# Seven products for the first group of two attention pairs, with its neighbours moved

## The chip, the cores and the metric

The kernel runs on one core of one Trainium2 chip. Its time is the device time of one execution in microseconds (us), the median of three runs. The core has a matrix engine (TensorE, "PE" in the profile; "PEld" is its weight load), a vector engine (VectorE, "DVE"), a scalar engine (ScalarE, "ACT"), GpSimd ("POOL") and SyncE ("SP"). ACT, DVE and POOL each take their instructions in the order of one queue. In this kernel SP and POOL also issue the transfers (DMA). PE accumulates in eight PSUM banks of 128 x 512 words.

## The reference

Two layers on 512 tokens of width 1024. Layer one is attention with eight heads of 128 in three groups of windows: group 0 looks back over 128 neighbouring tokens, group 1 over 128 tokens at distance 4, group 2 over 128 tokens at distance 16. Each group has its own q, k and v. The first 32 of the 128 dimensions of q and k are turned by position (rope). The three groups' outputs are joined with weights from their log sum of exponentials:

```
for g, (window, dilation) in enumerate(((128, 1), (512, 4), (2048, 16))):
    q = rope(proj[:, :, g, 0]) * scale;  k = rope(proj[:, :, g, 1]);  v = proj[:, :, g, 2]
    o, lse = dilated_window_attention(q, k, v, window, dilation)
wts = softmax(stack(lses), axis=0);  out = einsum(wts, stack(outs)) @ w_out
```

Then come a gated feed-forward layer, a recurrent mixer (mLSTM) with its own feed-forward layer, and a last norm. Only the attention of layer one is changed.

## The kernel before

Everything is float32. A float32 product is made of three matmuls in a rounded format: each operand is split into a high part, a rounded copy made by ScalarE (`split_chunk`, L223), and a low part, the remainder, made by VectorE (L225); then high x high, high x low and low x high are summed in PSUM (`SPLITS`). A block of weights is 128 x 1024 words, 512 KB. It is fetched into one of three buffers by SP, cast, and its remainder taken. Split blocks have four buffers, so a few blocks can be ready before PE needs them; `Feed` holds the list of blocks to come (`plan`) and those that are ready, and `feed.ahead` says how many.

Attention works on four pairs of heads (`pr` 0 to 3), and for each pair on the groups 0, 1, 2 in turn. For each, q and k of the two heads are projected from the normed input. There are two ways to do it:

- plain (`project`): q and k, each 2 blocks x 2 heads x 4 chunks x 3 matmuls, in all 96 matmuls of 512 columns;
- by seven products (`qk_unit`): the 2 x 2 block product of Strassen in Winograd's form. Sums of the input blocks (S1 to S4) are made once before. Each group then takes seven products of 24 matmuls of 256 columns, in the order P1, P5, P6, P2, P7, P3, P4 (`QK_ORDER`), on four differences of weight blocks (L879, made by VectorE in `prepare_part`) and with copies and sums of the results (L911 to L931).

Before the change, pair 0 is plain in all groups, pairs 1 to 3 have a plain group 0 and seven products in groups 1 and 2. In the program's names a2g0q is q of pair 2, group 0, and a2g1c, a2g1p, a2g1u are the accumulators of its group 1. Group 0 holds its q and k in an order by blocks of tokens, the other two in token order by classes.

After a group comes its turn by position (`rope`): the first 32 rows are packed on ACT (L905), turned on DVE (L607 to L616) and copied back (L628 by ACT for groups 1 and 2; POOL for group 0).

The attention of a pair (`attention_pair`) is cut into steps that run between the projections of later groups. A counter, the tick, is raised four times in every group (`advance`; in a group of products after P5, P2, P3 and P4), and `defer(n, fn)` puts a step n ticks on. So a pair of projections lasts twelve ticks. The steps, with their ticks before the change, counted from the start of the next pair's projections:

- `scores0` (group 0): 16 matmuls, masks and maxima on DVE (L709), exponentials on ACT (L753). It runs in its own pair, `SCORES0_AT` = 6 ticks after that pair's group 0, that is at tick 10, after P2 of group 2. Casts that are queued after it in the program are placed behind its exponentials on ACT (`ahead_of_casts`), low parts behind its last DVE instruction (`ahead_of_splits`).
- `scores12` (groups 1 and 2), tick 1: 32 matmuls, 16 masked maxima of 128 columns on DVE (L737), exponentials on ACT (L758).
- `joint`, tick 4: the three groups' maxima and sums are exchanged and joined into factors; `weigh(0)`, 4.5, and `weigh(1)`, 8: the probabilities of a head are multiplied by their factors on DVE (L802, L805), eight instructions each.
- `transposes(0)`, 5, and `transposes(1)`, 8; the results go to memory and come back (`bring`), 7 and 9.
- `values(0)`, 11, and `values(1)`, 12: 30 matmuls each (L829, L834), whose result is kept in memory by `keep_head`. `load_values` (2, 3 and 1) fetches the v that they need; it has one buffer.

The order on PE is fixed: `run` puts a step's matmuls together at its place, and the next product's matmuls follow it (`fenced`). On the other engines the instructions are placed by a planner, mostly in the order of the program, with the constraints named above. Pair 3 has no next pair: its steps run beside the projection of the last values (a3g12v, four blocks) by `LAST_AT`; then comes the output projection (awo), for which the kept heads 0 to 5 are fetched by `bring_heads`.

Of the kernel before, what the change touches and what calls it, by code (L numbers as in the profile page):

```python
# [35 lines left out]
SCORES0_AT = 6  # L36
RUN_AT = (1, (4, 4.5, 5, 7, 8, 8, 9), (11, 12), (2, 3, 1))
LAST_AT = (1, (2,), (), (1, 1, 1))
# [35 lines left out]
def tile_hybrid_dilated_attn_mlstm(  # L74
# [329 lines left out]
    with ExitStack() as actx:  # L404
# [9 lines left out]
        mask_band, mask_causal, mask_dil, perm = part(K_MA, 2 * P), part(K_M1, P), part(K_M2, P), part(K_G, P)  # L414
        cosn = ap.tile([P, SEQ], F32, name="cosn")
# [242 lines left out]
        def attention_pair(pr, qks):  # L658
# [35 lines left out]
            def scores0(q, k):  # L694
# [26 lines left out]
                else:  # L721
                    defer(2, lambda: behind(exps, engine=ACT))
# [3 lines left out]
            def scores12(gs=(1, 2)):  # L726

                for g in gs:
# [6 lines left out]
                for g, i in [e for e in ((1, 0), (2, 0), (1, 1), (2, 1)) if e[0] in gs]:  # L735
# [5 lines left out]
                    if g == 2:  # L741
                        exponentials(1, i)

            def exponentials(o, i):

                if o:
                    nc.vector.tensor_tensor(own[:, 0, 1, i], mx[:, 0, i], mx[:, 1, i], op=ALU.max)
# [49 lines left out]
            def weigh(i):  # L797
                cf4 = weight[0]
                for b in range(4):
                    pb = max(2 * b - 1, 0)  # L800
                    blk = p0[i][:, pb:2 * b + 1, :].rearrange("p a b -> p (a b)")
                    nc.vector.tensor_scalar(blk, blk, cf4[:, 0, i, b:b + 1], None, op0=ALU.mult)  # L802
                for c in range(4):
                    blk = p12[i].rearrange("p (g c) k -> p c g k", g=2)[:, c]
                    nc.vector.tensor_scalar(blk, blk, cf4[:, 1, i, c:c + 1], None, op0=ALU.mult)  # L805
# [58 lines left out]

        def load_part(pr, g, key):
            if g > 2:
                return
# [6 lines left out]
        def prepare_part(pr, g, name):  # L874
# [21 lines left out]
        def qk_unit(pr, g, qk):  # L896
# [7 lines left out]
            def pack(q, src):  # L904
                nc.scalar.activation(two_m(rot[0][quarter(q)]), src, AF.Copy)  # L905

            def finish(name):
# [8 lines left out]
                elif name in ("P2", "P4"):  # L916
                    th = int(name == "P4")
                    src = two_m(acc[target[name]])
                    if th == 0:
                        t = ap.tile([P, 2, SEQ], F32, tag="rot", name="rot")  # L920
                        rot = t[:, 0], t[:, 1]
                    pack(th, src[:R])
# [1470 lines left out]
```

## Time and profile before

| | |
|---|---|
| median of three runs | 1385.5 us (1385.12 to 1385.57) |
| the profiled execution | 1385.26 us, span of the trace 1383.5 us |
| attention's pairs 1, 2 and 3 (from the trace) | 179.6 to 255.7, 255.7 to 332.1, 332.1 to 410.05 us |
| last values, output projection | to 434.2, to 484.7 us |

Rows of the profile read as follows. A timeline row has the start in us from the start of the span, the duration, the engine, the line of the kernel, the operation, the tile written and the tiles read, the shape, how many were merged (x3), and in brackets how long the engine was idle before it and what ended that. A row of busy time by stretch has the stretch, its length, then for each engine its busy time and its number of instructions, then the granted clock of PE, the share of the transfer engines and GB/s. A row of a group by line has the number of instructions, their busy time, the mean duration of one in ns, and the idle time of the engine before them. PE's matmuls overlap one another: the distance from one start to the next is what a matmul costs, not its duration.

### The profile page before, as it was taken

What the parts mean: (1) busy time and instruction counts of PE and PEld (TensorE: products, weight loads), DVE (VectorE), ACT (ScalarE), POOL (GpSimd) and SP (SyncE); (2) the same over time, 40 slices, a digit from 0 to 9 for tenths busy, and PEclk for the clock granted to TensorE, in tenths of its full rate; (3) what the DMA queues carried; (4) which work ended last, traced back from release to release, by engine and by line L of the source; (5) the groups of instructions that cost most, each with busy time, mean ns of one, the idle gap of its engine ahead of it and who ended that gap; (6) DMA issues with size and microseconds to landing.
All of it is one profiled execution on the core that took longest, in us unless ns stands there. A gap on an engine that the chain in (4) does not pass through costs nothing. (4 is left out here: it accounts for less than half of the span.)

```text
span 1383.5 us, 22546 instructions
## 1 busy us (share of the span) xinstructions
PE 1368.5 (99%) x8740; PEld 1242.9 (90%) x8740; DVE 1111.3 (80%) x1845; ACT 780.5 (56%) x1246; POOL 180.2 (13%) x264
## 2 busy tenths in 40 slices
PE   9999999999999999999999999999999999999997
PEld 7888889899998889999999998898888999999886
DVE  7758769696896489788778798898858988887887
ACT  6556565656554354444476464695534454448854
POOL 3000013121211010000010110122102330001113
PEclk9999999999999999999999999999999999999999
DMA  8534255637286256323362742324335553335863
GB/s 298 176 120 139 77 153 161 197 122 237 91 280 205 102 137 183 111 73 122 122 153 77 168 124 80 103 66 119 92 122 124 156 173 105 122 122 129 192 167 100
DMA packets 140067, 193.81 MB, mean 140 GB/s; under 512 B 8980, under 2 KB 104788, under 8 KB 139960
## 3 DMA queue, kind: packets, MB, share of 16 engines
q1 hardware_dynamic: 119552, 139.81, 31.7%
q0 software_dynamic: 18752, 51.43, 15.7%
q8 instruction: 69, 1.13, 0.3%
q10 hardware_dynamic: 1656, 1.12, 0.2%
q14 instruction: 38, 0.31, 0.1%
HBM read 167.30 MB, written 22.54 MB: 137 GB/s over the span
## 5 line engine op out<-in xcount | busy, mean ns | idle before, releaser
L1696 POOL DMA_DIRECT2D f1T<-in_ffn_w_out_dram x15 | 17.8, 1185 | 208.7 <-DMA f1P_2w_w<-in_ffn_w_out_dram 135.7
L1671 POOL DMA_DIRECT2D f0S<-in_ffn_w_out_dram x10 | 8.7, 874 | 260.3 <-DVE f0hid L1588 173.1
L2228 POOL DMA_DIRECT2D hD<-hB x32 | 21.7, 697 | 68.3 <-DVE hB L2225 68.3
L255 PE MATMUL mo<-n_h,mo_k_l 128*128 128x512 f32 x64 | 25.3, 396 | 0.0
L255 PE MATMUL mo<-n_h,mo_k_h 128*128 128x512 f32 x64 | 25.3, 395 | 0.0
L255 PE MATMUL mo<-n_l,mo_k_h 128*128 128x512 f32 x64 | 25.2, 393 | 0.0
L255 PE MATMUL awo<-ao_h,awo_k_h 128*128 128x512 f32 x64 | 25.2, 393 | 0.0
L255 PE MATMUL mqk<-n_h,mqk_k_h 128*128 128x512 f32 x64 | 25.1, 392 | 0.0
L255 PE MATMUL mwo<-yo_l,mwo_k_h 128*128 128x512 f32 x64 | 25.1, 392 | 0.0
L255 PE MATMUL mqk<-n_l,mqk_k_h 128*128 128x512 f32 x64 | 25.1, 392 | 0.0
L255 PE MATMUL f0j<-n_h,f0j_h 128*128 128x512 f32 x64 | 25.0, 391 | 0.0
L255 PE MATMUL f1j<-n_h,f1j_h 128*128 128x512 f32 x64 | 25.0, 391 | 0.0
L255 PE MATMUL awo<-ao_h,awo_k_l 128*128 128x512 f32 x64 | 25.0, 391 | 0.0
L255 PE MATMUL mwo<-yo_h,mwo_k_l 128*128 128x512 f32 x64 | 25.0, 391 | 0.0
L255 PE MATMUL mqk<-n_h,mqk_k_l 128*128 128x512 f32 x64 | 25.0, 390 | 0.0
L255 PE MATMUL awo<-ao_l,awo_k_h 128*128 128x512 f32 x64 | 25.0, 390 | 0.0
L255 PE MATMUL f0j<-n_h,f0j_l 128*128 128x512 f32 x64 | 24.9, 390 | 0.0
L255 PE MATMUL f1j<-n_h,f1j_l 128*128 128x512 f32 x64 | 24.9, 390 | 0.0
L255 PE MATMUL f0j<-n_l,f0j_h 128*128 128x512 f32 x64 | 24.9, 389 | 0.0
L255 PE MATMUL f1j<-n_l,f1j_h 128*128 128x512 f32 x64 | 24.9, 389 | 0.0
L255 PE MATMUL mwo<-yo_h,mwo_k_h 128*128 128x512 f32 x64 | 24.8, 391 | 0.0
L225 DVE TENSOR_TENSOR v1P_l<-v1W,v1P_h 128x1024 fp32r<-128x1024 f32 x14 | 17.1, 1222 | 9.3 <-ACT v1P_h L223 9.3
(2613 smaller groups left out, 5875.7 us busy)
## 6 DMA issues: line engine op xcount, KB each, us to landing
f0j_w<-in_ffn_w_in_dram SPq DMA_DIRECT2D x17, 512.0 KB, 4.8
f1j_w<-in_ffn_w_in_dram SPq DMA_DIRECT2D x17, 512.0 KB, 6.4
f1T<-in_ffn_w_out_dram POOLq DMA_DIRECT2D x15, 512.0 KB, 7.0
f0hid<-in_ffn_w_in_dram SPq DMA_DIRECT2D x9, 512.0 KB, 5.2
f1hid<-in_ffn_w_in_dram SPq DMA_DIRECT2D x9, 512.0 KB, 4.8
v0W<-in_attn_w_in_dram SPq DMA_DIRECT2D x8, 512.0 KB, 6.1
v1W<-in_attn_w_in_dram SPq DMA_DIRECT2D x8, 512.0 KB, 3.5
awo_k_w<-in_attn_w_out_dram SPq DMA_DIRECT2D x8, 512.0 KB, 4.5
```

The lines of the kernel that those rows point to most:

```text
L225: nc.vector.tensor_tensor(lo[:, :n], raw[:, :n], hi[:, :n].bitcast(F32), op=ALU.subtract)
L255: nc.tensor.matmul(acc, whl[a][:, k, m * P:(m + 1) * P], pairs[b][kk], start=(kk == 0 and (a, b) == SPLITS[0]), stop=(kk == nk - 1 and (a, ...
L1671: nc.gpsimd.dma_start(t, src[1][:, ks], accum_op=ALU.add)
L1696: nc.gpsimd.dma_start(view(to), weight_rows(hk * UNITS + u, n), accum_op=ALU.add)
L2228: nc.gpsimd.dma_start(hD[k // 4].rearrange("(b i) x -> i b x", i=R)[:, :, c0:c0 + R], t[R * a_:R * (a_ + 1)])
```

## The change

Group 0 of pairs 2 and 3 is projected by seven products as well (`PRODUCTS_FROM = 2`, `by_products`). The weights of that group are fetched while group 2 of the pair before is prepared. Its results are written in the order by blocks, so each copy and sum is done once per head (`each`), its packed rows lie in two tiles of another pool, and the turned rows go back by POOL.

For all pairs but the last, `weigh(1)` runs on ACT instead of DVE, and at tick 7 instead of 8.

`scores12`, where it does both groups, takes the maximum over both groups at once (`both_groups`): eight instructions of 256 columns instead of sixteen of 128 and a maximum of the two; the exponentials follow after all of them. Pair 3 keeps the old way.

`scores0` runs one tick later, after P3 of group 2. The values run at 14.4 and 15.4, that is in the next pair's group 0 after P2 and P3 (for pair 2, beside the last values' projection), and `load_values` at 4, 5 and 4. In pair 3 the exponentials of `scores0` are put off by one tick instead of two, and heads 4 and 5 are fetched four ticks after heads 0 to 3.

```
-SCORES0_AT = 6
-RUN_AT = (1, (4, 4.5, 5, 7, 8, 8, 9), (11, 12), (2, 3, 1))
-LAST_AT = (1, (2,), (), (1, 1, 1))
+SCORES0_AT = 7
+RUN_AT = (1, (4, 4.5, 5, 7, 7, 8, 9), (14.4, 15.4), (4, 5, 4))
+PRODUCTS_FROM = 2
+LAST_AT = (1, (2,), (), (4, 4, 4))
...
-            for ks in (slice(0, 4), slice(4, 6)):
+            def bring_some(ks):
                 nc.sync.dma_start(t[:, ks], oD[ks].rearrange("k p s -> p k s"))
+            bring_some(slice(0, 4))
+            defer(4, lambda: bring_some(slice(4, 6)))
...
-                    defer(2, lambda: behind(exps, engine=ACT))
+                    defer(1, lambda: behind(exps, engine=ACT))
...
+            def both_groups():
+                for c2 in range(2):
+                    for i in range(2):
+                        sp = banks_[c2, i] = score_bank(i, "%ss12" % nm)
+                        for c in (2 * c2, 2 * c2 + 1):
+                            for g in (1, 2):
+                                q, k = qks[g]
+                                sl, o = slice(c * P, (c + 1) * P), (c % 2 * 2 + g - 1) * P
+                                nc.tensor.matmul(sp[:, o:o + P], q[:, i, sl], k[:, i, sl], start=True, stop=True)
+                two_g = lambda t: t.rearrange("p (g k) -> p g k", g=2)
+                for i in range(2):
+                    for c in range(4):
+                        nc.vector.tensor_tensor_reduce(
+                            p12[i].rearrange("p (g c) k -> p c g k", g=2)[:, c],
+                            two_g(banks_[c // 2, i][:, c % 2 * 2 * P:(c % 2 + 1) * 2 * P]), two_g(mask_both),
+                            1.0, -3e38, op0=ALU.add, op1=ALU.max, accum_out=own[:, 0, 1, i, c:c + 1])
+                ahead_of_splits[0] = last_on(DVE)
+                for i in range(2):
+                    exponentials(1, i)
...
+                def times(blk, f):
+                    if i and pr < HEADS // 2 - 1:
+                        nc.scalar.activation(blk, blk, AF.Copy, scale=f)
+                    else:
+                        nc.vector.tensor_scalar(blk, blk, f, None, op0=ALU.mult)
...
+        def by_products(pr, g):
+            return pr > 0 and (g > 0 or pr >= PRODUCTS_FROM)
...
             if g > 2:
+                pr, g = pr + 1, 0
+            if pr == HEADS // 2:
                 return
...
+            follows = g < 2 or pr + 1 >= PRODUCTS_FROM
             if name == "P7":
                 less("W21", "W21", "W11")
                 for key in ("W11", "W12"):
-                    load_part(pr, g + 1, key)
-            elif name in ("P3", "P4"):
+                    if follows:
+                        load_part(pr, g + 1, key)
+            elif name in ("P3", "P4") and follows:
                 load_part(pr, g + 1, src)
...
+            def each(out, src, th, fn):
+                if g:
+                    fn(halves(out, th), *(two_m(t) for t in src))
+                    return
+                for m in range(2):
+                    at = slice(m * HALF, (m + 1) * HALF)
+                    fn(in_order(out[:, m])[:, :, 2 * th:2 * th + 2],
+                       *(t[:, at].rearrange("p (c b j) -> p b c j", c=2, b=TB) for t in src))
...
-                    pack(th, src[:R])
-                    nc.scalar.activation(halves(qk[0], th), src, AF.Copy)
+                    pack(th, two_m(src[:R]))
+                    each(qk[0], [src], th, lambda to, x: nc.scalar.activation(to, x, AF.Copy))
...
-                    pack(2 + th, out[:R])
+                    if g:
+                        pack(2 + th, halves(qk[1], th)[:R])
+                    else:
+                        for m in range(2):
+                            nc.scalar.activation(packed(rot, 2 + th, m, True), turned(qk, 2 + th, m, True), AF.Copy)
...
-                if pr and g:
+                if by_products(pr, g):
                     qk.extend(tok_tile("%sg%d_%s" % (nm, g, "qk"[part])) for part in range(2))
-                    qk_unit(pr, g, qk)
+                    qk_unit(pr, g, qk, then if g == 0 else None)
                     continue
```

More of the change, by code (lines that the diff above doesn't have):

```diff
@@ L414, in tile_hybrid_dilated_attn_mlstm @@
         mask_band, mask_causal, mask_dil, perm = part(K_MA, 2 * P), part(K_M1, P), part(K_M2, P), part(K_G, P)
+        mask_both = part(K_M1, 2 * P)
         cosn = ap.tile([P, SEQ], F32, name="cosn")
@@ L967, in qk_unit @@
                 if n == 6 and not last:
-                    back = rope(qk, rot, False)
-                    if g == 2:
+                    back = rope(qk, rot, g == 0)
+                    if g == 0:
+                        defer(1, lambda: back(True))
+                    elif g == 2:
                         back()
@@ L975, in qk_unit @@
                     advance()
+                if n == 6 and then is not None:
+                    then()
                 if n:
@@ L1240, in tile_hybrid_dilated_attn_mlstm @@
             for g, part, ch in itertools.product(range(3), range(2), range(2)):
-                if pr and g:
+                if by_products(pr, g):
                     if (part, ch) == (0, 0):
```

25 lines of the change are left out of this document (15 added, 10 removed).

## The prediction

> **What bounds the kernel now.** I read the page first, then busy time by stage for pair 2, then the timelines of PE, ACT and DVE there, and last the groups by line.
>
> ```profile
> span 1383.5 us, 22546 instructions
> ...
> PE 1368.5 (99%) x8740; PEld 1242.9 (90%) x8740; DVE 1111.3 (80%) x1845; ACT 780.5 (56%) x1246; POOL 180.2 (13%) x264
> ```
>
> PE is busy 99% of the span, so time goes only where PE does less or waits more. The chain of waits on the page covers the end of the kernel alone and does not reach attention. The profiled execution took 1385.26 us, 0.24 below the median of 1385.5; I sum against it and add that back. Pair 2 by group (length, then PE, PEld, DVE, ACT, POOL):
>
> ```profile
> 255.70:281.50 25.80, 25.80 (x132) 21.88 (x132) 17.16 (x59) 14.86 (x33) 3.17 (x5) 1.00 0.45 133
> 281.50:301.60 20.10, 20.10 (x170) 20.09 (x169) 20.00 (x35) 11.16 (x15) 7.86 (x12) 1.00 0.47 151
> 301.60:332.10 30.50, 30.18 (x246) 29.47 (x245) 23.13 (x43) 19.99 (x39) 4.99 (x9) 1.00 0.67 206
> ```
>
> The rows are group 0 (plain), group 1 and group 2 (seven products), at clock 1.00. VectorE is full in group 1 (20.00 of 20.10) and has 8.6 us free in group 0, just where the change puts work. PE's existing stalls on the other engines are small:
>
> ```profile
> 249.69 0.39 PE L959 MATMUL a1g2u<-xa_h,a1g2P_l 128*128 128x256 f32 x1 [0.24 <-DVE a1g2P_l L225]
> ```
> ```profile
> 304.89 0.38 PE L959 MATMUL a2g2p<-S,a2g2P_h 128*128 128x256 f32 x1 [0.31 <-ACT a2g_q L923]
> ```
>
> The first is a low part made late, because its cast stood behind the exponentials of scores0. The second is a copy out of PSUM that stood on ACT behind a cast that waited. Both are queue order, not throughput; this decides my forecast.
>
> **Part 1, group 0 by products.** What PE does in the group beside it:
>
> ```profile
> 261.23 3.74 PE L734 MATMUL a1s<-a1g_k,a1g_q 128*128 128x128 f32 x32
> 264.72 0.48 PE L255 MATMUL a2g0q<-xa_h,a2g0q_k_h 128*128 128x512 f32 x1
> ```
> ```profile
> 278.50 0.38 PE L770 MATMUL a1xps<-a1ex,acst 128*128 128x128 f32 x2
> 278.63 0.48 PE L255 MATMUL a2g0k<-xa_h,a2g0k_k_h 128*128 128x512 f32 x1
> ```
>
> Scores12 take 264.72 - 261.23 = 3.49 us, the exchange 0.13. The plain group is thus 25.80 - 3.62 = 22.2 us for 96 matmuls of 512 columns; group 1 does 168 of 256 columns in 20.1. Each break in the stream costs the matmul after it some 0.1 (0.48 against 0.39 busy), and group 0 will have three: 20.4. PE gains 1.8 per group, **-3.6 us** for pairs 2 and 3. Bounds: -4.2 (no breaks) and -2.7 (if a break costs 0.25). [...]
>
> What the other engines get, from the groups by line of pair 2:
>
> ```profile
> L225 DVE TENSOR_TENSOR a2g1P_l<-a2g1W,a2g1P_h 128x1024 fp32r<-128x1024 f32 x7 | 8.7, 1250 | 3.4 <-ACT a2g1P_h L223 3.4
> ...
> L879 DVE TENSOR_TENSOR a2g1W<-a2g1W,a2g1W 128x1024 f32<-128x1024 f32 x4 | 4.9, 1220 | 0.0
> ...
> L737 DVE CUSTOM_DVE_ANT_0 a1p<-a1s,acst 128x128 f32<-128x128 f32 x16 | 3.6, 283 | 0.0
> L709 DVE CUSTOM_DVE_ANT_0 a2p<-a2s,acst 128x256 f32<-128x256 f32 (+1 forms) x8 | 2.8, 389 | 0.6 <-PE a2s L703 0.5
> ...
> L802 DVE TENSOR_SCALAR a1p<-a1p,a1cf 128x256 f32<-128x256 f32 (+1 forms) x8 | 2.4, 348 | 0.0
> ...
> L805 DVE TENSOR_SCALAR a1p<-a1p,a1cf 128x256 f32<-128x256 f32 x8 | 2.3, 343 | 0.0
> ...
> L1010 DVE COPY a2g_k<-a2g0k 128x512 f32<-128x512 f32 x2 | 1.4, 685 | 0.0
> ...
> L931 DVE TENSOR_TENSOR a2g_k<-a2g2p,a2g2vu 128x512 f32<-128x512 f32 x1 | 0.7, 692 | 2.1 <-PE a2g2p L959 2.1
> ```
> ```profile
> L223 ACT ACTIVATE a2g1P_h<-a2g1W 128x1024 fp32r<-128x1024 f32 x7 | 7.4, 1057 | 3.1 <-DVE a2g1W L879 2.6 <-PE a2g0k L255 0.4
> ...
> L758 ACT ACTIVATE a1p<-a1p,a1nb 128x256 f32<-128x256 f32 x8 | 4.0, 496 | 3.9 <-DVE a1nb L748 3.9
> ```
>
> VectorE: three more splits and four block differences, 3 x 1.25 + 4 x 1.22 = +8.6; four copies go, -2.8; four half-width adds come, between 0.35 (half of 0.69) and 0.69, I take 0.4: +1.6. **Part 2**, the second head weighed on ScalarE: half of 2.4 + 2.3, -2.35. **Part 3**, eight maxima of 256 instead of 16 of 128: 8 x 0.39 = 3.1 at most against 3.6, -0.5. Net +4.5 per pair on 60.3 (sum of the three rows): 64.8 of some 74.6 us, 87%. ScalarE: three casts +3.2, about 15 small copies instead of 8 +3.2, weighing 8 x 0.50 = 4.0 at most: 46.0 to 56.4, 76%. Neither becomes the bound by its sum. These costs lie beside PE's matmuls; their cover is the lookahead of three to four products, 2.87 us each (20.1 / 7), and group 0 is now 20.4 + 3.6 + 6.5 of values = 30.5 us long, so it refills it. I cost them at nothing, but take **-0.5** for the two stalls quoted, whose causes (exponentials ahead of the last cast of group 2; weighing on VectorE in group 1) move away; bounds 0 and -1.0.
>
> **Part 4, what is moved, and where it lands.** Values leave the end of group 2 for group 0 of the next pair (for pair 2: for the closing value projection, a3g12v); scores0 come one step later, after the sixth product instead of the fourth. PE's matmuls are the same, but between scores0 and the next scores12 there is less PE work to hide a chain on DVE and ACT. The chain today, at the end of pair 2 (PE, then ACT, then DVE):
>
> ```profile
> 313.88 0.60 PE L703 MATMUL a2s<-a2g_k,a2g_q 128*128 128x128 f32 x3
> ...
> 316.73 0.47 PE L959 MATMUL a2g2u<-S3h,a2g2P_h 128*128 128x256 f32 x1
> ...
> 328.84 1.72 PE L829 MATMUL a1o<-a1pT,a1v 128*128 128x128 f32 x14
> ...
> 332.10 0.48 PE L255 MATMUL a3g0q<-xa_h,a3g0q_k_h 128*128 128x512 f32 x1
> ...
> 337.67 0.72 PE L734 MATMUL a2s<-a2g_k,a2g_q 128*128 128x128 f32 x5
> ```
> ```profile
> 318.01 0.40 ACT L753 ACTIVATE a2p<-a2p,a2nb 128x128 f32<-128x128 f32 x1 [2.81 <-DVE a2nb L748]
> ...
> 321.75 1.04 ACT L223 ACTIVATE a2g2P_h<-a2g2W 128x1024 fp32r<-128x1024 f32 x1
> ...
> 329.04 0.59 ACT L905 ACTIVATE rot<-a2g2u 32x512 f32<-32x512 f32 x1 [1.32 <-PE a2g2u L959]
> 329.65 0.60 ACT L923 ACTIVATE a2g_q<-a2g2u 128x512 f32<-128x512 f32 x1
> 332.54 1.27 ACT L628 ACTIVATE a2g_q<-rot 32x512 f32<-32x512 f32 x2 [2.29 <-DVE rot L616]
> 333.83 1.28 ACT L628 ACTIVATE a2g_k<-rot 32x512 f32<-32x512 f32 x2
> ```
> ```profile
> 329.67 0.73 DVE L607 STREAM_SHUFFLE rot<-rot 128x512 f32<-128x512 f32 x1
> ```
>
> Count from the start of scores0. Their exponentials end at 321.75 - 313.88 = 7.9, and the code puts every later cast behind them. After the change the next operand prepared is the difference product (P5) of the next pair's group 0: cast to 8.9, low part (1.25) to 10.1. PE reaches it after scores0 (2.85), the last product and P1 (2 x 2.87), at 8.6, its first low part some 0.25 later: it waits **1.3**. Then scores12 need the turned q and k of group 2. Today that chain runs from 329.04 to the first k copy, 333.83 + 0.64 = 334.47, 5.4 us, and scores12 come 3.2 us after it (337.67), since the values (332.10 - 328.84 = 3.26) and a plain chunk lie between. After the change the packing stands on ACT behind exponentials and cast, at 8.9, and the shuffle behind that low part, at 10.1 instead of 9.5: k is there at 14.9. PE has done P5 at 10.1 + 2.6 = 12.7 and waits up to 2.1. If the packing goes ahead of the cast, P5 waits longer (about 2.5 in all) and scores12 do not. I take 2.8 at each of the two boundaries (pairs 1 to 2, 2 to 3), **+5.6**. Bounds: 0 (ACT's order spreads the packing between the exponentials and the chain fits) and 4.8 each (3.2 plus a wait like the 1.65 below, if stores are late for scores0 again). No gain is possible here, since no work goes.
>
> ```profile
> 242.14 0.29 DVE L709 CUSTOM_DVE_ANT_0 a1p<-a1s,acst 128x128 f32<-128x128 f32 x1 [1.65 <-DMA a0pD<-a0pB]
> ```
>
> The end of pair 3 loses the same cover:
>
> ```profile
> 398.81 0.38 PE L829 MATMUL a2o<-a2pT,a2v 128*128 128x128 f32 x2
> ```
> ```profile
> 412.89 0.50 PE L734 MATMUL a3s<-a3g_k,a3g_q 128*128 128x128 f32 x3
> ```
> ```profile
> 409.77 0.68 DVE L613 TENSOR_TENSOR a3g_q<-rot 32x512 f32<-32x512 f32 x1
> ```
>
> From the sixth product's end (398.81) the scores of group 2 start 14.1 later; DVE has turned q 11.6 later (410.45), 2.4 to spare. In the changed order PE arrives 6.5 earlier for the values and 2.9 later for scores0, at 10.5, and DVE has scores0's 3.0 more in that stretch, less what it idles there. A wait between 0 and 3; I take **+0.5**, near 0, because this pair's exponentials do not hold its casts.
>
> At nothing: the loads of values on POOL's queue move two to four steps; they wait there for PE's last use of the old values, now just done, and the copies of turned q and k behind them are due only at scores0, over 30 us later. Values have 60 us. The fetch of heads 4 and 5 (SP queue, four steps later) waits for their store; behind it stand the weights' fetches of the output projection, and heads 4 and 5 are multiplied only after a3g12v and three blocks of four heads (24 matmuls each), over 20 us after the last values. The weight blocks of the new group 0 are fetched as those of group 2 are, 2 MB either way.
>
> **Sum.** -3.6 - 0.5 + 5.6 + 0.5 = +2.0: 1387.3 for such a profiled execution, **1387.5** as a median. That is inside 0.2% (2.8 us), about what a measurement of this kernel can tell from no change.
>
> **Rivals.** *The cover holds.* ACT interleaves packing and exponentials so that neither P5 nor scores12 wait. For it: PE had only 0.5 us of waits in three pairs. Against: casts are held by an explicit order. Then -4.1: 1381.4. With half the waits it is -1.3.
> *VectorE runs dry in group 2*, ending slower. Without the values group 2 is 30.5 - 6.5 = 24.0 us long, and of its 23.1 us of VectorE only the last turn (about 2.7) moves out while a block difference (1.2) comes in: 21.6, 90%, with two waits of some 2 us for PE (the 2.1 in the add's row) in an in-order queue. It decides once the lookahead brought from groups 0 and 1 falls under one product (2.9 us); then each of three pairs pays about 1.5: +2.0 + 4.5, 1392.0. Weighing on ScalarE feeds it, since the second transpose waits for it. [...]
> *Heads 4 and 5 late in the closing stage*: their store, today 5.1 us to landing, wholly in the open.
>
> ```profile
> oD<-o_keep POOLq DMA_DIRECT2D x2, 256.0 KB, 5.1
> ```
>
> That gives 1392.6; against it stand the three blocks counted above.
>
> **How the numbers follow.** Forecast as summed (net -1 to +4): 0.44; cover holds: 0.30; VectorE dry: 0.20; late heads: 0.06. The range 1381.2 to 1391.6 leaves out the outer halves of the side cases, about 2 in 10; the likeliest case alone is 1384.5 to 1389.5. Faster by over 0.2% are four fifths of "cover holds": 0.24. Slower are a third of the forecast, VectorE dry and late heads: 0.40. Within: 0.36.
>
> **What would show it.** Right: group 0 of pairs 2 and 3 has 168 matmuls of 256 columns; PE rows with an idle time before the third matmul of P5 (released by the low part, L225's line) and before the second or third matmul of scores12 (released by the copy back, L628's line), 1 to 3 us per pair; ACT with exponentials, cast, packing in that order. Wrong: no such PE wait and group 0 near 30.5 us (cover holds); PE waiting for low parts all through groups 1 and 2 (VectorE dry); plain groups gone but group 0 over 20.6 us of matmuls (part 1 mis-sized).

## The result and the profile after

The changed kernel takes 1401.6 us (median of four runs, 1400.7 to 1402.1) where the kernel before takes 1385.45: 1.0114 times as long, 95% interval 1.0102 to 1.0127. It is slower by 16 us, and well outside the predicted range. Line numbers below are those of the changed kernel (L224 cast, L226 low part, L630 copy back of turned q and k, L714 maxima of scores0, L781 and L786 the exponentials, L1017 the products' matmuls); runs that insert lines shift those behind by a few. The page:

```profile
span 1400.3 us, 22832 instructions
...
PE 1373.7 (98%) x8884; PEld 1253.7 (90%) x8884; DVE 1120.2 (80%) x1781; ACT 798.0 (57%) x1286; POOL 182.9 (13%) x264
```

PE is busy 5.2 us more although it has fewer columns to do, and its idle time grows from 15.0 to 26.6 us. Where, three stretches show, cut at PE's first matmul of a group: group 2 of pair 1 with group 0 of pair 2; the same one pair later with group 1 ahead of it; and from group 1 of pair 3 to the output projection. Columns are the stretch, its length, then busy time of PE, PEld, DVE, ACT, POOL, the granted clock, the DMA share and GB/s. Before:

```profile
225.47:281.51 56.04, 55.80 (x377) 51.36 (x375) 40.32 (x103) 34.82 (x72) 8.15 (x14) 1.00 0.56 169
281.51:358.02 76.51, 76.19 (x543) 71.48 (x542) 60.46 (x136) 46.11 (x87) 16.01 (x26) 1.00 0.52 162
358.02:434.17 76.15, 76.07 (x543) 71.42 (x542) 67.59 (x156) 45.72 (x86) 16.68 (x28) 1.00 0.63 204
```

After:

```profile
225.34:286.01 60.67, 56.74 (x448) 56.00 (x447) 44.53 (x80) 39.64 (x79) 6.92 (x13) 0.94 0.43 138
286.01:368.92 82.91, 76.75 (x617) 75.57 (x616) 65.10 (x115) 53.25 (x103) 17.04 (x27) 0.96 0.48 150
368.92:451.53 82.61, 78.97 (x545) 73.33 (x544) 71.74 (x163) 47.99 (x94) 20.75 (x34) 0.98 0.67 213
```

They grow by 4.6, 6.4 and 6.5 us, and the granted clock, 1.00 before, is below 1 in each. PE's waits of the changed kernel, from 176 to 500 us (what waited, for what, us in all, times, longest):

```profile
PE a3g0p L1017 <- ACT a3g0P_h L224: 5.4, 1, 5.4
PE a2g0p L1017 <- ACT a2g0P_h L224: 3.2, 1, 3.2
PE a3xps L798 <- DVE a3ex L793: 2.6, 1, 2.6
PE a2g0p L1017 <- DVE a2g0P_l L226: 0.7, 1, 0.7
PE a3g0p L1017 <- DVE a3g0P_l L226: 0.5, 1, 0.5
```

So the place is the predicted one, P5 of the next pair's group 0, but the wait is 3.9 and 5.9 us instead of 1.3, and a third stands at the joint factors of pair 3. With two of 0.4 and 0.2 at pair 3's scores, and two of 0.3 in group 1 of pairs 2 and 3, they make 13.6 us; the kernel before has 0.5 in the same stretch. The rest is what follows a wait. The 3.4 us that begin 0.3 us after the first wait's end, two more such steps, and P5 of pair 3:

```profile
255.00:258.40 3.40, 2.67 (x13) 2.47 (x12) 2.31 (x3) 3.33 (x6) 0.00 (x0) 0.50 0.00 0
258.41:261.82 3.41, 3.41 (x18) 3.41 (x17) 3.41 (x4) 2.94 (x5) 0.00 (x0) 0.50 0.00 0
261.83:265.20 3.37, 3.37 (x32) 3.37 (x31) 3.34 (x15) 0.76 (x2) 0.00 (x0) 1.00 0.65 179
...
338.46:344.22 5.76, 5.30 (x24) 5.00 (x25) 4.68 (x4) 5.30 (x7) 0.00 (x0) 0.54 0.00 0
```

At each of the two boundaries the granted clock is 0.50 for 6.8 us, and P5's 24 matmuls hold PE for 5.3 to 5.4 us (3.2 where the clock stays at 1.00, in the second run below). That is a cost of its own, about 2 to 3 us at each boundary and 1.6 at the end (the first head's values behind the third wait take 4.9 us, the second's 3.3). The sum: 13.6 of waits, less the 0.5 of before, some 6.4 of low clock, less some 3 that PE gains, makes 16.5. The three stretches grew by 17.5 us and the span by 16.8.

What held P5's cast, at the boundary from pair 2 to 3: first PE's scores0 and VectorE's last row on their maxima for the first head, then ScalarE in order of time (start, duration, in brackets the idle time and what ended it):

```profile
324.12 3.20 PE L708 MATMUL a2s<-a2g_k,a2g_q 128*128 128x128 f32 x16
```
```profile
328.54 0.16 DVE L776 TENSOR_SCALAR a2nb<-a2own 128x4 f32<-128x4 f32 x1
```
```profile
330.22 0.59 ACT L946 ACTIVATE rot<-a2g2u 32x512 f32<-32x512 f32 x1 [3.42 <-PE a2g2u L1017]
330.83 0.60 ACT L977 ACTIVATE a2g_q<-a2g2u 128x512 f32<-128x512 f32 x1
333.15 0.58 ACT L1005 ACTIVATE a3g0u<-a3g0c 128x512 f32<-128x512 f32 x1 [1.72 <-PE a3g0c L1017]
333.65 0.39 ACT L781 ACTIVATE a2p<-a2p,a2nb 128x128 f32<-128x128 f32 x1
...
337.36 1.04 ACT L224 ACTIVATE a3g0P_h<-a3g0W 128x1024 fp32r<-128x1024 f32 x1
```

ScalarE takes the packing and the copy of P4, then idles until PE ends P1, to copy its sum (L1005), then does the exponentials, then P5's cast, which begins 4.3 us after PE has finished P1 (at 338.46 - 5.40 = 333.06). The exponentials could have begun at 328.7, 4.6 us after scores0, against 4.1 in the kernel before. The 4.9 us that they are late are 1.5 until P4's end, 1.2 of packing and copy, 1.7 until P1's end and 0.5 for the copy of its sum. At the boundary from pair 1 to 2 (scores0 begin at 242.56) it is a late weight block instead, which ScalarE waits for (`a2g0P_h`, P1's cast) and behind which VectorE's low part, an addition and then the maxima stand:

```profile
244.32 1.06 ACT L224 ACTIVATE a2g0P_h<-a2g0W 128x1024 fp32r<-128x1024 f32 x1 [2.71 <-DMA a2g0W<-in_attn_w_in_dram]
...
249.84 0.40 ACT L781 ACTIVATE a1p<-a1p,a1nb 128x128 f32<-128x128 f32 x1
```
```profile
245.41 1.23 DVE L226 TENSOR_TENSOR a2g0P_l<-a2g0W,a2g0P_h 128x1024 fp32r<-128x1024 f32 x1 [4.47 <-ACT a2g0P_h L224]
...
247.15 0.28 DVE L714 CUSTOM_DVE_ANT_0 a1p<-a1s,acst 128x128 f32<-128x128 f32 x1
```

The maxima begin 4.6 us after scores0 there, where the other boundary has 1.9.

The third wait has the same form: pair 3's exponentials stand on ScalarE behind a weight cast that waits 5.2 us for its block, so the sums they deliver are late for the exchange.

```profile
420.89 1.06 ACT L224 ACTIVATE a3g12v_k_h<-a3g12v_k_w 128x1024 fp32r<-128x1024 f32 x1 [5.24 <-DMA a3g12v_k_w<-in_attn_w_in_dram]
421.86 0.38 ACT L781 ACTIVATE a3p<-a3p,a3nb 128x128 f32<-128x128 f32 x1
```

### The profile page after: what moved, and what is told of

It reads as the page before. It is cut to its first block, busy times and chain, and to the rows that moved or that the text cites. A ratio compares the mean times of both kernels' runs of the same rounds, so it can differ in the third digit from the quotient of the medians.

```text
span 1400.3 us, 22832 instructions
## 1 busy us (share of the span) xinstructions
PE 1373.7 (98%) x8884; PEld 1253.7 (90%) x8884; DVE 1120.2 (80%) x1781; ACT 798.0 (57%) x1286; POOL 182.9 (13%) x264
## 5 line engine op out<-in xcount | busy, mean ns | idle before, releaser
L226 DVE TENSOR_TENSOR awo_k_l<-awo_k_w,awo_k_h 128x1024 fp32r<-128x1024 f32 x8 | 9.8, 1224 | 19.0 <-ACT awo_k_h L224 19.0
```

What stands on the lines that cost most here:

```text
L226: nc.vector.tensor_tensor(lo[:, :n], raw[:, :n], hi[:, :n].bitcast(F32), op=ALU.subtract)
```

## The experiments

Each run is given with its time, or as a ratio with its interval against the kernel before on the same chip.

**First round: order, products, moves, clock.**

*Exponentials of scores0 one step later in every pair.*

```
-                if pr < HEADS // 2 - 1:
+                if pr < 0:
                     exps()
```

> Edit: the exponentials of scores0 are issued one step later for every pair (as the change has it for pair 3 alone), so that the cast for the next pair's difference product P5 no longer stands behind them on ScalarE. Theory A (the order on ScalarE makes the loss): PE's idle before P5 falls from 3.2 + 0.7 and 5.4 + 0.5 us to under 1 us each, the granted clock stays at 1.0 after it, which gives back 3.9 + 5.9 us of waits and about 3 us twice of half clock: 1401.6 - 15.8 = 1386 (1384 to 1390). Rival B (seven products are too much for VectorE and for the weights' fetch): PE waits as long for the low part or the weights, 1399 to 1402. Rival C (the moved values and scores are what costs): PE waits elsewhere instead, 1395 or more.

1402.7 us, no gain. PE's waits of 1 us and more for the casts of P5 and P6:

```profile
PE a2g0u L1017 <- ACT a2g0P_h L224: 2.1, 1, 2.1
PE a3g0u L1017 <- ACT a3g0P_h L224: 2.1, 1, 2.1
PE a3g0p L1017 <- ACT a3g0P_h L224: 1.7, 1, 1.7
```

The exponentials now stand ahead of P6's cast (tile `u`) and PE waits there; the wait at pair 3's joint factors is 3.7. That is what Rival C named. Theory A was too simple: what is put off by one place holds the next.

*The wait filled with idle matmuls*: `spin` puts 14 and 23 matmuls of 512 columns on PE, into a bank that nobody reads; the 14 keep PE busy for 3.4 us.

```
...
+                if name == "P5" and g == 0:
+                    spin({2: 14, 3: 23}[pr])
```

> [...] If the half clock after the wait is a cost of its own, set off by the idle time: the clock stays at 1.0 there, P5 takes 2.9 to 3.5 us instead of 6.1 and 5.8, and the time falls by about 3 us at each boundary, 1401.6 - 6 = 1395.6 (1394.5 to 1397). If the low clock comes from something else (the products themselves, the power drawn before), or is only how the records show a wait: no gain, 1401 to 1403.

1397.2 us, 4.4 faster and just outside the range, with P5's operand as late as before. P5 of pairs 2 and 3:

```profile
255.16:259.14 3.98, 3.22 (x24) 3.02 (x25) 2.89 (x4) 3.91 (x6) 0.00 (x0) 1.00 0.00 0
...
336.33:340.31 3.98, 3.22 (x24) 3.02 (x25) 2.90 (x3) 3.91 (x6) 0.00 (x0) 1.00 0.00 0
```

The clock stays at 1.00 and P5 holds PE for 3.2 us (in pair 3 it was 5.3). PE's waits there are 0.2 and 0.8 us in pair 2 and 0.8 in pair 3, where the change has 3.2 and 0.7, 5.4 and 0.5. So in these two runs the low clock (0.50 in the change) goes with the idle time, and it has a price of its own, the 4.4 us.

*The moves alone, and the products alone.*

```
-PRODUCTS_FROM = 2
+PRODUCTS_FROM = 4
```

> Edit: the change with the first groups of pairs 2 and 3 plain as before; the second head on ScalarE, the maxima by class and all moved steps stay. Theory A: without P5 behind the exponentials the two boundary waits go; plain group 0 costs 3.6 us more of PE; the wait in the closing value projection (2.6 us and 1.7 us of half clock) stays: 1385.5 + 4 to 5 = 1390 (1387 to 1393). Rival B (products are too much for VectorE): 1385 to 1387, no loss left. Rival C (the moves alone cost): 1398 or more.

```
-SCORES0_AT = 7
+SCORES0_AT = 6
-RUN_AT = (1, (4, 4.5, 5, 7, 7, 8, 9), (14.4, 15.4), (4, 5, 4))
+RUN_AT = (1, (4, 4.5, 5, 7, 8, 8, 9), (11, 12), (2, 3, 1))
...
-LAST_AT = (1, (2,), (), (4, 4, 4))
+LAST_AT = (1, (2,), (), (1, 1, 1))
...
-                    defer(1, lambda: behind(exps, engine=ACT))
+                    defer(2, lambda: behind(exps, engine=ACT))
```

> Edit: the change with every moved step back where it was (scores0 after the fourth product of group 2, values at the end of group 2, loads as before); products in group 0 of pairs 2 and 3, the second head on ScalarE and the maxima by class stay. Theory A: the exponentials are through before P5's cast is due, no wait over 1 us, PE's gain of 3.6 us is seen: 1385.5 - 3.6 = 1382 (1380 to 1385). Rival B: VectorE or the weights run late in any place, 1395 or more. Rival C: also 1382, so this run tells B from the two others, and the run of the moves alone tells A from C.

In both, the second head stays on ScalarE and the maxima over both groups stay. The moves alone take 1390.5 us (1.0036, 1.0025 to 1.0048), as Theory A had it. Two of their waits are those the prediction feared, scores12 for the copy back of k (a third, of 1.6, is the one at pair 3's joint factors):

```profile
PE a2s L762 <- ACT a2g_k L630: 1.4, 1, 1.4
PE a1s L762 <- ACT a1g_k L630: 1.4, 1, 1.4
```

The products alone take 1400.5 us, where 1382 was expected: a clear miss, and in favour of Rival B. Group 1 of pair 2 there:

```profile
282.84:306.78 23.94, 21.86 (x171) 21.69 (x170) 23.16 (x39) 16.03 (x28) 9.17 (x12) 0.93 0.45 130
```

VectorE is busy 23.16 of 23.94 us, 3 us more than in the change's group 1 (20.2 of 20.7): a low part, a block difference and an add more run there, arrears of a group 0 that lasts 26.3 us without the values. PE's other waits are 2.2 us in pair 2's group 0 and 2.0 and 0.8 in its group 2, for ScalarE and VectorE, 2.1 and 0.8 in pair 3's groups 1 and 0, and 2.3 for pair 2's probabilities on their way back from memory. So neither half is free. By these rows the products need the values' cover in group 0, and taking the values from the end of group 2 uncovers the boundary; no run tests the two apart from the weighing on ScalarE, which both have.

**Second round: more cover at the boundary, and the end.**

*Values right behind group 2; lookahead of three; both.*

```
-RUN_AT = (1, (4, 4.5, 5, 7, 7, 8, 9), (14.4, 15.4), (4, 5, 4))
+RUN_AT = (1, (4, 4.5, 5, 7, 7, 8, 9), (12, 12.4), (4, 5, 4))
```

> Edit: the change with the values of a pair at 12 and 12.4 steps instead of 14.4 and 15.4, so that they stand right behind the last product of group 2 (for pair 2, at the start of the closing value projection); scores0 stay where the change has them. Between scores0 and P5 PE then has 6.5 us more to do. Theory A2 (after the first runs: the stretch from scores0 to scores12 asks more of ScalarE than PE's work there covers; whatever is put last there waits): the waits of 3.9 and 5.9 us fall to at most 0 and 2.7, the half clock behind them goes (3 us twice), and the joint factors of pair 3 get 6.5 us more too (2.6 + 1.5 us): 1401.6 - 9.8 + 1.5 - 6 - 4 = 1383 (1381 to 1388). Rival B2 (VectorE has too little room in groups 0 and 1 once the values leave the middle of group 0, as in the run of the products alone): new waits in group 1 of pairs 2 and 3, 1392 or more.

```
-                if g == 2 and n == 2:
-                    feed.ahead = 2
```

> Edit: the change without the line that cuts the lookahead from three operands to two after the third product of group 2, so that P5's cast is issued before the exponentials of scores0. If the short lookahead is the cause: all boundary waits and half clock go, 1401.6 - 16 = 1386. Theory A2: the wait passes on to P6, as in the run with the later exponentials; with one more operand ready some of it is hidden: 1391 to 1400.

> Edit: both at once, the values at 12 and 12.4 and the lookahead of three kept. Theory A2: what is left at the boundary of pairs 2 and 3 goes too, PE's gain of 3.6 us is seen, 1381 to 1384. Rival B2: as for the values first, 1392 or more.

They take 1394.5, 1401.8 and 1405.0 us. Theory A2 missed all three, and the second lies outside both of its ranges; the first and the third are on Rival B2's side. With the values first, P5 waits no more, but the values do, 3.2 us, for the maxima of scores0's second head, with whose scores they share two PSUM banks in the code; and group 1 waits 2.1 for VectorE, as Rival B2 said:

```profile
PE a1o L863 <- DVE a2own L714: 3.2, 1, 3.2
PE a2g1u L1017 <- DVE a2g_k L985: 2.1, 1, 2.1
```

With three operands ahead P5 is on time and scores12 wait instead, for the copies back on ScalarE, 5.1 and 3.4 us:

```profile
PE a1s L762 <- ACT a1g_k L630: 5.1, 1, 5.1
...
PE a2s L762 <- ACT a2g_k L630: 3.4, 1, 3.4
```

Pair 3's scores wait 4.9 us for maxima besides. With both at once the values wait 6.6, 4.2 and 3.2 us for maxima.

*The joint factors of pair 3 behind one head's values.*

```
-LAST_AT = (1, (2,), (), (4, 4, 4))
+LAST_AT = (1, (2.45,), (), (4, 4, 4))
```

> Edit: the change with the joint factors of pair 3 at step 2.45 instead of 2 of the closing value projection, that is behind the first head's values of pair 2 instead of ahead of them: 2.9 us more of PE work between the scores and the exchange. If the end's 2.6 us wait and the half clock behind it (3.4 us at 0.5, some 1.5 us lost) are a cost of their own: 1401.6 - 4 = 1397.5 (1396.5 to 1399). If the last projection waits for pair 3's values later instead: 1401 to 1403.

1397.8 us: 3.8 faster, as expected; the 2.6 us wait and its low clock are gone (mean granted clock 0.995, in the change 0.992).

**Third round: exponentials where nobody waits for them; the small parts.**

*Two steps later, and behind scores12* (both with the later joint factors).

```
-                if pr < HEADS // 2 - 1:
+                if pr == 0:
                     exps()
...
-                    defer(1, lambda: behind(exps, engine=ACT))
+                    defer(1 if pr == HEADS // 2 - 1 else 2, lambda: behind(exps, engine=ACT))
```

> Edit: the change with the exponentials of scores0 of pairs 1 and 2 two steps later (behind P5's cast, the turned q and k's copies and P6's cast), and the joint factors of pair 3 at step 2.45. Theory A3 (after eight runs: at the boundary ScalarE owes PE the packing, two casts and the turned copies before scores12, and the exponentials are the only thing there that nobody waits for; wherever they stand ahead of one of the others PE waits for it): no PE wait over 1 us at the two boundaries, no half clock, no wait at the end: 1401.6 - 9.8 - 6 - 4 = 1382 (1380 to 1386), faster than before. If the boundary lacks work on PE whatever the order: waits pass on to scores12 or P6 once more, 1390 or more.

The second writes 2.5 instead of 2.

> Edit: as the run before, with the exponentials of scores0 behind those of scores12 (2.5 steps later). Theory A3: the same at the boundary, but the joint factors have less time behind both sets of exponentials: between 1381 and 1387. If it is slower by over 4 us than the two-steps kernel, the place of the exponentials within group 0 matters too.

1391.8 and 1393.3 us: beside the run with the later joint factors alone (1397.8) the exponentials bring 6.0 and 4.5, and 10 are missing of what was expected of the first; the second misses its range too. The boundary from pair 1 to 2 is mended (group 0 takes 32.87 us instead of 37.57, at clock 1.00), the other is not (37.37). VectorE there:

```profile
326.71 0.01 DVE L609 LOAD_MASK_SELECT rot<-rot  x1 [4.71 <-ACT rot L946]
326.71 0.73 DVE L609 STREAM_SHUFFLE rot<-rot 128x512 f32<-128x512 f32 x1
327.35 0.27 DVE L714 CUSTOM_DVE_ANT_0 a2p<-a2s,acst 128x128 f32<-128x128 f32 x1
```

The shuffle that turns group 2 stands ahead of the maxima and waits 4.7 us for P4's packing; the maxima, and the block difference for P5 that the code puts behind them, stand in its queue.

*Second head back on VectorE; maxima by group.*

```
-                    if i and pr < HEADS // 2 - 1:
+                    if False:
```

> Edit: the change with the weighing of the second head back on VectorE (eight multiplications per pair). If VectorE in group 1 was near its limit (20.2 of 20.7 us busy), its 2.35 us more per pair come out as PE waits for low parts or for k's add there, 2 to 3 us for each of pairs 1 to 3: 1403 to 1409. If the lookahead hides it, as the prediction costed the weighing at nothing: 1401 to 1402.5.

```
-                if len(gs) == 2:
-                    both_groups()
-                    return
```

> Edit: the change with scores12 and their maxima by group as before (16 maxima of 128 columns instead of 8 of 256, a separate maximum of the two). By the prediction's working that is 0.5 us of VectorE per pair, hidden: 1401 to 1402. If the two groups' order matters (the scores of group 1 need nothing of the last rope and can begin before it): up to 3 us faster, 1398.5 to 1401.

1403.3 and 1402.5 us. Weighing on VectorE costs 1.7 us by the medians, less than the 2 to 3 for each of three pairs, and little more than these runs can tell (1.0113 to 1.0145 against 1.0102 to 1.0127 for the change); the maxima cost or give less than they can tell. Neither part makes the loss.

**Fourth round: the order written out.** The "mended order" is the two-steps kernel with the turning behind the maxima; the same edit was made in the change alone, and the mended order was run with plain first groups and with a lookahead of three.

```
-                    back = rope(qk, rot, g == 0)
+                    with behind_scores() if g == 2 else nullcontext():
+                        back = rope(qk, rot, g == 0)
```

> Edit: as the run with the exponentials two steps later and the joint factors later, and the turning of q and k of group 2 (its shuffle first) issued behind the maxima of scores0 on VectorE. In that run VectorE stood 4.7 us idle in front of the shuffle with the maxima, ready on PE's side, queued behind it, at the boundary from pair 2 to 3 alone, which took 37.4 us (start of its group 0 to start of group 1) where the other took 32.9. Theory A4 (VectorE's order is the other half of the cause): P5's 3.3 us wait and its half clock go, both stretches take 32 to 33 us: 1391.8 - 4.5 = 1387.3 (1385 to 1389). If P5 waits there for another reason: 1390 to 1392.

> Edit: the change as it is, with that order of VectorE alone (the turning of group 2 behind the maxima of scores0). Theory A4: VectorE's order and the exponentials each hold P5's cast; with the maxima at their due time the exponentials end about 8 us after scores0 began, as in the kernel before, and P5 waits the 1.3 us of the prediction or up to 3: 1401.6 - 2 - 4 and up to - 6 of half clock: 1390 to 1396. If the exponentials alone are the cause: 1400 to 1402.

> Edit: as the mended kernel (exponentials two steps later, joint factors later, turning behind the maxima), with the first groups of pairs 2 and 3 plain as before. The two kernels of one order tell what the products themselves are worth: by the prediction's first part this one is 3.6 us slower than the mended one, 1390 to 1392 where that is at 1387; if products cost more on the other engines than PE gains, it is the faster one, under 1387.

> Edit: as the mended kernel, with the lookahead of three operands kept through group 2. If P5's operand is still what PE waits for in the mended one (0.9 + 0.7 us where it was first seen), it is ready now: 1384 to 1386. If ScalarE has no room before scores12, the wait goes there again, as in the run with the lookahead alone (5.1 and 3.4 us): 1390 or more.

1392.7, 1402.3, 1385.0 and 1401.8 us: all four fall on the side of the alternative that was named with them, so Theory A4 is at most a part of it. The second could give little: in the change VectorE turns group 2 behind the maxima already (the shuffle at 330.85, the maxima from 326.06 on), the edit only moves P5's block difference ahead of the shuffle, and ScalarE's order, with the copy of P1's sum and the exponentials ahead of P5's cast, stays. In the first, the boundary from pair 2 to 3 falls from 37.37 to 34.94 us. But the one from pair 1 to 2 rises from 32.87 to 34.23, since waits of nearly the same length (0.8 and 0.9 us, there 0.7 and 0.9) are followed by half clock this time (0.95 over the stretch, there 1.00; the last section has the rows), pair 3's scores now wait 2.1 for maxima that stand behind that pair's last shuffle, and P5 still waits 1.7, for this:

```profile
326.82 0.60 ACT L977 ACTIVATE a2g_q<-a2g2u 128x512 f32<-128x512 f32 x1
329.14 0.58 ACT L1005 ACTIVATE a3g0u<-a3g0c 128x512 f32<-128x512 f32 x1 [1.72 <-PE a3g0c L1017]
329.63 1.05 ACT L224 ACTIVATE a3g0P_h<-a3g0W 128x1024 fp32r<-128x1024 f32 x1
```

P5's cast stands behind the copy of P1's sum, the instruction already seen ahead of the exponentials. The plain groups in the same order (third) have no wait over 0.4 us: 1385.0, level with the kernel before. So in one order the products cost 7.6 us: 5.6 more of waits and three steps of low clock (3.4 us at 0.50, about 1.7 lost in each; two by the boundaries' 0.95, the third an estimate from the mean clock, 0.995 against 0.998), less the 3 that PE gains. The fourth passes the wait on, as the lookahead alone did: 4.8 and 4.4 us in front of scores12 and 4.8 at pair 3's scores.

*The copy behind P5's cast, and pair 3's last shuffle behind its maxima; then the same with products in pair 3 alone.*

`p5_cast` keeps P5's cast when it is issued.

```
...
-                    nc.scalar.activation(acc["u"], acc["c11"], AF.Copy)
+                    with tc.issue_after(p5_cast[nm]) if g == 0 else nullcontext():
+                        nc.scalar.activation(acc["u"], acc["c11"], AF.Copy)
...
-                        rope(qk, rot, False, 1, 2, True)
+                        with behind_scores():
+                            rope(qk, rot, False, 1, 2, True)
```

> Edit: as the mended kernel (exponentials two steps later, joint factors later, turning behind the maxima), and two orders more: ScalarE's copy of P1's sum behind P5's cast (at the boundary from pair 2 to 3 the copy stood ahead of the cast, and ScalarE idled 1.7 us for P1's end in front of it), and the last turning of pair 3 behind its maxima. Theory A5 (what remains is the order of single instructions around the chain maxima, difference, cast, low part, each wait with half clock behind it): P5's 1.7 + 0.8 us of pair 3 fall under 1 us without half clock (-1.8 - 1.5), the scores of pair 3 no longer wait 2.1 us (-2.1 - 1.5): 1392.7 - 6.9 = 1385.8 (1384 to 1389); the boundary from pair 1 to 2 keeps its 1.7 us and its half clock, since there P1's weights land late (ScalarE idle 3.0 us for them). If the waits pass on again: 1390 or more.

The second sets `PRODUCTS_FROM = 3` besides.

> Edit: as the kernel with the copy behind the cast, with group 0 by products in pair 3 alone (pair 2 plain). Theory A5: the boundary from pair 1 to 2 is then as in the mended order with plain groups (32.5 us from the start of group 0 to the start of group 1), that of pair 3 gains PE's 1.8 us less a wait of up to 1 us: 1385.0 - 1 = 1384 (1382.5 to 1385.5), level with the kernel before or just faster. If the products cost at any boundary: 1386 or more.

1386.9 (1.0012, 1.0003 to 1.0021) and 1385.0 us (0.9996, 0.9987 to 1.0005): both inside the ranges of Theory A5, but not in every part. The half clock that was expected to stay at the boundary from pair 1 to 2 in the first did not come. In the second P5 of pair 3 waits 1.7 us, where the late weight block is now (ScalarE idles 2.98 us for it), and the stretch takes 33.00 us, no less than the 32.57 of the plain group. The first has taken 14.7 us off the change by the order of instructions alone; in its trace the clock is 1.00 in both boundary stretches and 0.999 over the span, as in the kernel before. What the products are worth with few waits left is seen between the plain groups 0 of pairs 2 and 3 in the mended order,

```profile
248.58:281.10 32.52, 32.52 (x192) 28.54 (x191) 20.25 (x49) 20.26 (x53) 4.84 (x8) 1.00 0.34 106
324.25:356.82 32.57, 32.57 (x192) 28.53 (x191) 19.60 (x49) 20.15 (x52) 4.84 (x8) 1.00 0.32 97
```

with group 1 of pair 2 behind the first

```profile
281.10:301.18 20.08, 20.08 (x169) 20.08 (x168) 19.47 (x29) 13.50 (x23) 7.85 (x12) 1.00 0.59 190
```

and the groups 0 by products (the copy behind the cast), with the group 1 behind each:

```profile
248.82:281.90 33.08, 31.25 (x264) 30.66 (x263) 26.64 (x58) 25.30 (x59) 3.61 (x7) 1.00 0.29 91
325.97:357.34 31.37, 30.98 (x265) 30.58 (x263) 24.02 (x45) 25.27 (x59) 3.58 (x7) 1.00 0.36 114
...
281.90:302.90 21.00, 20.36 (x172) 20.19 (x170) 20.82 (x36) 13.92 (x25) 10.75 (x14) 1.00 0.69 201
357.34:378.36 21.02, 20.40 (x172) 20.23 (x171) 20.82 (x36) 13.81 (x25) 10.81 (x14) 1.00 0.67 200
```

PE has 1.3 and 1.6 us less to do in group 0. Pair 2 loses it to the 1.8 us that P5 still waits there; pair 3 keeps 1.2. Then each loses 0.9 to 1.0 in group 1 (pair 3's takes 20.04 us in the mended order with plain groups), where VectorE is now busy 20.8 of 21.0 us and PE waits 0.6 for it. No version run beats the kernel before; two are level with it.

## Why the prediction was wrong

**The step that failed** is Part 4, "I take 2.8 at each of the two boundaries": P5's wait of 1.3 was measured at 3.9 and 5.9. Its mechanism was right (P5's cast behind the exponentials of scores0), its count was not: it carried over from the trace of before that the exponentials end 7.9 us after scores0 begin. In the changed kernel they end 11.0 and 13.2 us after. The sentence "If the packing goes ahead of the cast, P5 waits longer (about 2.5 in all)" named the order that came, but priced only the packing. What came with it, with everything on ScalarE standing ahead of the exponentials, was 1.5 us of idle time until P4's end, 1.7 until P1's end for the copy of its sum, and the two copies; at the other boundary a late weight block (2.7). The second half of that term, scores12 waiting up to 2.1 for k, did not happen in the change, because P5 had waited already; with plain groups it did, at 1.4.

**A term was missing**, put at nothing without a word: the granted clock. Some 6.4 us of the 16 are matmuls at half speed (clock 0.50) behind the waits. The rows of before, all at 1.00, could not show it; the run with the filled wait gives 4.4 us of it back.

**The end of pair 3**, "+0.5 (0 to 3)", was 3.2 us of waits and 1.6 of low clock. The wait is not the one looked at (scores of group 2 for the turned q, 0.4) but the exchange behind late exponentials.

**Part 1**, -1.8 per group, is about right for PE (1.3 to 1.6). That its cost on VectorE would be covered ("I cost them at nothing") holds in the change, where group 1 has waits of 0.3 only. Once the waits at the boundary are gone, VectorE takes 0.9 to 1.0 us a pair in group 1. Of parts 2 and 3, costed at nothing, the weighing on ScalarE is worth about 1.7 us (its undoing costs that, near the limit of what the runs tell) and the maxima nothing that can be told.

**The rivals.** The cover did not hold. "VectorE runs dry in group 2" does not happen in the change, whose group 2 has no wait; the products alone show that engine run dry in group 1. Heads 4 and 5 are on time. The case that came, the forecast's own mechanism at more than twice its price (waits and low clock make 6.6 and 8.0 us at the two boundaries), was in no rival, and the upper bound of "4.8 each" was set by waits alone.

Of **what would show it**, the idle time before P5's low part is there (0.7 and 0.5), but the long one is ahead of P5's first matmul, for the cast; the idle time inside scores12 is not; and ScalarE's order is packing, exponentials, cast, not exponentials, cast, packing.

Left open: why the order of the single instructions came out so. The runs show which instruction stood in front of which and what it cost, not how the order was chosen. The late weight block was not mended in any run: it stands at the boundary from pair 1 to 2, and from pair 2 to 3 where pair 2 is plain, so in each case at the first group 0 by products. Why it lands late there is not shown.

## What to carry to other kernels

When a change takes matmuls away from between two dependent stages, list every instruction that the engines beside PE still owe there, in queue order, and ask of each what it waits for: a copy that waits for PE itself, put ahead of an operand's cast, makes PE wait for its own result (ScalarE idled 1.7 us for P1's end here), which no busy share shows. Price a wait of PE with what follows it: two waits of 1.7 us in all cost as much again where half clock followed, and those of 3.9 and 5.9 us two to three more. And measure a part in the order that suits it before judging it: against plain groups (1385.0) the products cost 7.6 us in one order and 1.9 in another, with the same work.

## What the runs showed of the hardware

In the change the granted clock falls to 0.50 and comes back to 1.00 at 255.01 and 261.83 us, 336.93 and 343.75, 432.50 and 435.91. These times lie 2, 22, 2, 26 and 1 times 3.41 us apart, so its trace can be cut into such steps, and the busy time of PE read for each. The step ahead of each fall, and the steps at half clock:

```profile
251.60:255.01 3.41, 0.34 (x2) 0.30 (x2) 3.38 (x6) 3.41 (x12) 0.00 (x0) 1.00 0.00 0
255.01:258.42 3.41, 2.68 (x13) 2.50 (x12) 2.32 (x3) 3.34 (x6) 0.00 (x0) 0.50 0.00 0
258.42:261.83 3.41, 3.41 (x18) 3.41 (x17) 3.41 (x4) 2.94 (x5) 0.00 (x0) 0.50 0.00 0
333.51:336.93 3.42, 0.00 (x0) 0.00 (x0) 2.28 (x3) 3.42 (x16) 0.00 (x0) 1.00 0.01 2
336.93:340.34 3.41, 1.42 (x5) 1.12 (x6) 1.86 (x2) 3.36 (x8) 0.00 (x0) 0.50 0.00 0
340.34:343.75 3.41, 3.41 (x18) 3.41 (x18) 2.37 (x3) 3.38 (x4) 0.00 (x0) 0.50 0.00 0
429.09:432.50 3.41, 0.80 (x6) 0.58 (x6) 1.08 (x5) 2.52 (x11) 0.00 (x0) 1.00 0.47 154
432.50:435.91 3.41, 3.41 (x19) 3.41 (x18) 2.87 (x15) 2.21 (x4) 0.00 (x0) 0.50 0.00 0
```

Half clock follows steps in which PE was busy for 0.34, 0.00 and 0.80 us. Up to 1376 us this trace has 393 other steps at full clock, all followed by full clock; PE is busy least in this one:

```profile
951.33:954.74 3.41, 2.44 (x12) 1.75 (x11) 2.26 (x9) 2.07 (x12) 0.74 (x2) 1.00 0.81 222
```

Of the five steps at half clock, the two in which PE was busy for 2.68 and 1.42 us were followed by another, the three in which it was busy throughout by full clock.

Much shorter waits were followed by half clock in another run, though not always. In the mended order P5 of pair 2 waits 0.8 and 0.9 us, both in one step, and the next is at half clock:

```profile
251.08:254.49 3.41, 1.69 (x12) 1.34 (x11) 3.38 (x7) 1.38 (x2) 0.00 (x0) 1.00 0.00 0
254.49:257.90 3.41, 3.41 (x18) 3.41 (x17) 2.50 (x3) 3.02 (x5) 0.00 (x0) 0.50 0.00 0
```

With the copy behind the cast the waits there are nearly the same, 0.9 and 0.9, but they lie in two neighbouring stretches of a step's length, PE is busy for 73% of both, and the clock stays at 1.00:

```profile
249.50:252.92 3.42, 2.51 (x21) 2.31 (x20) 3.42 (x13) 1.98 (x4) 0.00 (x0) 1.00 0.01 4
252.92:256.33 3.41, 2.49 (x20) 2.28 (x21) 3.37 (x5) 1.04 (x3) 0.00 (x0) 1.00 0.00 0
```

So in these rows the half clock goes with how little PE did within one step, more than with the length of a wait. That the second trace's steps begin at 249.50 and 252.92 us is the author's reading: no fall of its clock marks them there. By that reading the half clock that did not come with the copy behind the cast, about 1.7 us, is owed to where the steps fell in that execution and not to the order of instructions; this was not shown, as no run moved one wait along the steps.
